# Norm factor kept in PSUM, half 1's product beside it, one set of PSUM banks with fixed homes at the passages, mask cast on ScalarE

## The chip, the cores and the metric

The kernel runs on one core of a Trainium2 chip. Its engines each work through their own queue of instructions in order: TensorE (PE, matrix products; its weight loads are listed as PEld), VectorE (DVE), ScalarE (ACT), GpSimd (POOL) and SyncE (SP, which issues the DMAs). The metric is the device time of one execution in microseconds (us); the median of several executions is compared.

## The reference

One inference step of a two-layer backbone on 640 tokens (128 context tokens, 512 latent ones) of width 1024. Layer 0 is an FFN half-step, a mixer (windowed attention beside a gated linear attention, one input and one output projection) and another FFN half-step; layer 1 is an FFN half-step, a chunked gMLP mixer and another FFN half-step. Each sub-layer is wrapped alike, and it is this wrapping that the change touches:

```python
def rmsnorm(x, g):
    xf = x.astype(jnp.float32)
    y = xf * lax.rsqrt(jnp.mean(xf * xf, axis=-1, keepdims=True) + EPS)
    return (y * g.astype(jnp.float32)).astype(x.dtype)

def sub_in(x, mod, i, g_pre):
    return rmsnorm(x, g_pre) * (1 + mod[:, i, 1][:, None]) + mod[:, i, 0][:, None]

def sub_out(x, y, mod, i, g_post, coef):
    return x + coef * mod[:, i, 2][:, None] * rmsnorm(y, g_post)

def macaron_ffn(x, mod, i, g_pre, g_post, wg, wu, wd):
    h = sub_in(x, mod, i, g_pre)
    y = (jax.nn.silu(h @ wg) * (h @ wu)) @ wd
    return sub_out(x, y, mod, i, g_post, FFN_RESIDUAL)
```

So between the last product of one sub-layer and the first of the next stand a norm of y, a gated addition to x, a norm of x and a scaling.

## The kernel before

The activations x and y lie transposed in SBUF, 128 partitions by 8 chunks (KD) of 1024 features by 640 tokens. The tokens are cut into two halves: half 0 has 384, half 1 has 256, and these are two pieces of 128 with different gates (context and latent). Products are made in full precision from split operands: an activation is hh + hl, a weight tile whl holds its rounded value and the rest, and each 128x128 piece takes three matmuls (hh and hl with the rounded weight, hh with the rest). Weights stream from HBM through two raw buffers, are cast by ACT (line 100) and their rest is made by DVE (line 101). All code is recorded and put in order by a list scheduler, engine by engine, so the order on an engine isn't that of the text.

From one sub-layer to the next ("passage") the work is this. `tail` makes the last products and evacuates them into y; `chain`, once for each half, makes the norm factor (`rstd`: a matmul with ones sums the squares, ACT takes Ln and Exp), then for each chunk runs three stages, each one step behind the other: `f_t` multiplies y by gate and factor in place (line 428), `f_x` adds y to x (line 464) and has ACT make hh (line 435), `f_l` makes hl on DVE (line 440). Squares of the new x and a second `rstd` follow. `head` makes four products jointly (`gemm_joint`, chunk by chunk over four PSUM banks) for half 0 while the chains run, evacuates each as a product with the norm factor (`normed`, line 606), makes the later products, and does the same for half 1. Ahead of a mixer `renorm` normalises x once more, with the same helper (line 428, reading x) and hh, hl at lines 494 and 498.

PSUM has eight banks of 128 x 512 floats. Outside of the passages `ps()` takes from a ring of eight. `split_psum` closes the pool and opens one with two rings of four, "ps" and "sd" (with four dummy matmuls); `whole_psum` in `head` closes that again and opens a ring of eight, right before the joint products of half 1, so the first of these must wait until every bank of the old pool has been read. Two of the five passages (after out_proj) have no split: there the ring of eight stays.

Five passages are spoken of: P1 into mixer 0 (about 480 to 525 us), P2 from out_proj into the next FFN (857 to 902), P3 into layer 1's first FFN (1300 to 1342), P4 into mixer 1 (1742 to 1790) and P5 from its out_proj into the last FFN (1948 to 1995). In P1 the DVE queue also holds the cast of a mask for the mixer (line 901) and memsets (line 882).

Of the kernel before, what the change touches and what calls it, by code (L numbers as in the profile page):

```python
# [8 lines left out]
F32 = mybir.dt.float32  # L9
# [3 lines left out]
AF = mybir.ActivationFunctionType  # L13
# [4 lines left out]
P = 128  # L18
# [120 lines left out]
class Kern:  # L139
# [18 lines left out]
    def ps(self):  # L158
        if self.spare:
            return self.sd()  # L160
        return self.pp.tile([P, 512], F32, name=self.nm("ps"), tag="ps", bufs=8 - self.n_sd)

    def sd(self):

        return self.pp.tile([P, 512], F32, name=self.nm("sd"), tag="sd", bufs=self.n_sd)

    def open_psum(self, n_sd=0):
        self.n_sd, self.spare = n_sd, False
        self.g_ps = self.tc.tile_pool(name=self.nm("psum"), bufs=8, space=PSUM)
        self.pp = self.g_ps.__enter__()  # L170
# [12 lines left out]

# [267 lines left out]
    def chain(self, half, cur, nxt):  # L451
# [3 lines left out]
        o, n = HALF[half]  # L455
        self.rstd(half, 0, late=half == 1)
        yield

        def f_t(m):
            self.scaled(half, self.y, *cur, 2, m)  # L460

        def f_x(m):
            xs = self.x[:, m, o:o + n]
            nc.vector.tensor_add(xs, xs, self.y[:, m, o:o + n])  # L464
            if nxt is None:
                nc.sync.dma_start(out=self.O["x"][:, m, o:o + n], in_=xs)
            else:
                self.h_hi(half, *nxt, m)
# [12 lines left out]
        self.rstd(half, 2 if half and nxt != (0, 1) else 0, late=True)  # L481
        yield
# [48 lines left out]
    def tail(self, unit, n_blocks, cur, nxt, mod=()):  # L531
# [17 lines left out]
        for m in range(both, KD):  # L549
            unit(m, 1, wis)  # L550
            if nxt is not None:
                ws.pump(wis[-1] + (m + 1) * n_blocks // KD - both)
            st = min(11 - done, 1 if nxt is not None else LAST_STEPS[m])
            self.step(ch[0], st)
            done += st
        self.step(ch[0], 11 - done)
        return ch

    def head(self, ch, n_a, joint, unit, evac, nxt=None):
# [13 lines left out]
        for i in range(10):  # L573
            self.step(ch[1], 1)
# [277 lines left out]
    def mixer0(self, ch):  # L852
# [18 lines left out]
        def evac1(i, half, ps):  # L871
# [932 lines left out]
```

## Time and profile before

| | |
|---|---|
| time, three executions | 2420.77, 2416.78, 2415.56 us; median 2416.78 |
| the profiled execution | 2414.18 us, span 2412.4 us, mean granted clock 0.987 |
| busy share of the span | PE 96%, PEld 94%, DVE 77%, ACT 54%, POOL 14% |
| busy us | PE 2325.1, DVE 1851.1, ACT 1298.3, POOL 331.2 |
| chain that ended last, by engine | PE 74%, DVE 16%, DMA 4%, ACT 3%, issue 2%, POOL 1% |

PE is the engine on which the time lies; a busy share is an average over stages, and the stretches in which PE stands are short. They are found in the list of waits, placed by the timeline, and then the queue of the engine that PE waited for is read in the same stretch.

### The profile page before, as it was taken

The numbers are of one execution on the slowest core, as the hardware profiler recorded it, in microseconds if no ns is written. First come the engines' busy times: TensorE is split into PE (matmuls) and PEld (weight loads), VectorE is DVE, ScalarE is ACT, GpSimd is POOL, SyncE is SP. The second block draws the span as 40 slices with busy tenths as digits, with TensorE's granted clock in tenths as the row PEclk, the third lists the DMA queues.
The fourth block names the chain that finished last, engine by engine and source line by source line (L and its number), as shares of the span: only waits on it lengthen the run. The fifth ranks groups of instructions, "written<-read, shape, count | busy, mean of one in ns | idle before, by whom it ended". The sixth has DMA issues, their size and how long they took to land.

```text
span 2412.4 us, 40072 instructions
## 1 busy us (share of the span) xinstructions
PE 2325.1 (96%) x15528; PEld 2265.1 (94%) x15528; DVE 1851.1 (77%) x3315; ACT 1298.3 (54%) x2669; POOL 331.2 (14%) x289
## 2 busy tenths in 40 slices
PE   7899999989999999999999899999989999999998
PEld 5799999989898899999999899999978899999998
DVE  8888888795956698887886688787794787765574
ACT  4565455565446456554556465455573356554555
POOL 5200000140503330000004000000131540000002
PEclk9999999999999999999999999999999999999999
DMA  8333544431030343353543333443434343332322
GB/s 300 97 114 127 171 158 133 169 129 60 10 92 31 135 136 109 129 168 103 175 129 134 105 114 127 145 149 109 169 128 138 116 133 108 108 114 68 100 97 105
DMA packets 87569, 297.85 MB, mean 123 GB/s; under 512 B 9681, under 2 KB 15313, under 8 KB 84305
## 3 DMA queue, kind: packets, MB, share of 16 engines
q1 hardware_dynamic: 86082, 292.07, 37.2%
q8 instruction: 121, 1.98, 0.3%
q10 hardware_dynamic: 864, 2.17, 0.3%
q0 software_dynamic: 432, 1.05, 0.2%
q14 instruction: 70, 0.57, 0.1%
HBM read 276.25 MB, written 19.01 MB: 122 GB/s over the span
## 4 chain that ended last, share of the span: by engine, by line
PE 74%; DVE 16%; DMA 4%; ACT 3%; issue 2%; POOL 1%; SPq 0%; DVEq 0%; ACTq 0%; POOLq 0%
PE ps L201 38%; PE sd L201 35%; DVE hl L440 2%; DVE junk L328 2%; DVE whl L101 2%; DVE y L428 2%; DVE x L464 1%; DMA wmod<-in_wmod 1%; DMA b<-xspill 1%; ACT whl L100 1%; DMA wraw<-in_wgu 1%; DMA cbc<-in_cc 1%; DVE dm L369 1%; DVE tmp L606 0%; DVE cv L1419 0%
## 5 line engine op out<-in xcount | busy, mean ns | idle before, releaser
L201 PE MATMUL ps<-hh,whl 128*128 128x320 f32 (+4 forms) x4080 | 941.0, 315 | 38.2 <-DVE tmp L606 30.5
L101 DVE TENSOR_TENSOR whl<-wraw,whl 128x1024 fp32r<-128x1024 f32 (+3 forms) x552 | 532.8, 970 | 294.9 <-ACT whl L100 283.1
L201 PEld LDWEIGHTS ps<-hh,whl 128*128 128x128 f32 x4080 | 701.7, 191 | 43.6 <-ACT tmc L405 12.1
L201 PE MATMUL ps<-hl,whl 128*128 128x320 f32 (+4 forms) x2040 | 637.0, 312 | 16.1 <-DVE hl L440 14.7
L100 ACT CAST whl<-wraw 128x1024 fp32r<-128x1024 f32 (+3 forms) x552 | 462.2, 839 | 337.8 <-issue 124.2
L201 PE MATMUL sd<-g,whl 128*128 128x384 f32 (+1 forms) x3264 | 480.6, 308 | 0.3 <-DVE g L687 0.3
L201 PEld LDWEIGHTS sd<-g,whl 128*128 128x128 f32 x3264 | 477.0, 188 | 2.8 <-DVE g L687 1.1
L412 POOL TENSOR_TENSOR acc<-acc,tmc 128x384 f32<-128x384 f32 (+1 forms) x154 | 178.2, 1159 | 1748.8 <-ACT tmc L405 1735.6
L201 PEld LDWEIGHTS ps<-hl,whl 128*128 128x128 f32 x2040 | 391.5, 192 | 21.5 <-DVE hl L440 16.9
L201 PE MATMUL sd<-th,whl 128*128 128x320 f32 x2448 | 381.4, 308 | 1.3 <-ACT sd L690 1.1
L201 PEld LDWEIGHTS sd<-th,whl 128*128 128x128 f32 x2448 | 364.8, 187 | 2.1 <-ACT sd L690 1.6
L328 DVE SCALAR_TENSOR_TENSOR junk<-wmod,cbc 128x1024 bf16<-128x1024 f32 x258 | 326.7, 1266 | 30.8 <-DMA wmod<-in_wmod 20.4
L201 PE MATMUL sd<-hh,whl 128*128 128x320 f32 (+1 forms) x592 | 144.1, 314 | 0.0
L201 PEld LDWEIGHTS ps<-g,whl 128*128 128x128 f32 x960 | 140.0, 188 | 1.5 <-issue 1.5
L201 PE MATMUL ps<-g,whl 128*128 128x384 f32 (+1 forms) x960 | 140.8, 308 | 0.0
L826 ACT COPY y<-sd 128x384 f32<-128x384 f32 (+1 forms) x192 | 80.6, 424 | 103.5 <-PE sd L201 103.3
L201 PEld LDWEIGHTS sd<-hh,whl 128*128 128x128 f32 x592 | 101.9, 188 | 0.6
L435 ACT ACTIVATE hh<-x,dm 128x128 fp32r<-128x128 f32 (+1 forms) x144 | 63.3, 468 | 62.8 <-DVE x L464 43.9
L428 DVE SCALAR_TENSOR_TENSOR y<-y,dm,rstd 128x128 f32<-128x128 f32 (+1 forms) x128 | 70.7, 584 | 32.0 <-ACT rstd L399 32.0
L440 DVE SCALAR_TENSOR_TENSOR hl<-x,dm,hh 128x128 fp32r<-128x128 f32 (+1 forms) x144 | 90.2, 656 | 2.1 <-ACT hh L435 1.8
L201 PE MATMUL sd<-hl,whl 128*128 128x320 f32 (+1 forms) x296 | 91.3, 308 | 0.0
L797 ACT COPY sd<-y 128x384 f32<-128x384 f32 (+1 forms) x192 | 81.1, 434 | 17.2 <-DVE tmp L701 14.1
(251 smaller groups left out, 2599.2 us busy)
## 6 DMA issues: line engine op xcount, KB each, us to landing
wraw<-in_wgu SPq DMA_DIRECT2D x170, 512.0 KB, 3.7
wmod<-in_wmod SPq DMA_DIRECT2D x130, 512.0 KB, 4.1
wraw<-in_wd SPq DMA_DIRECT2D x64, 320.0 KB, 3.2
xspill<-x SPq DMA_DIRECT2D x12, 1280.0 KB, 4.5
x<-xspill SPq DMA_DIRECT2D x12, 1280.0 KB, 8.6
wraw<-in_wd SPq DMA_DIRECT2D x32, 384.0 KB, 3.8
wraw<-in_wdl SPq DMA_DIRECT2D x24, 512.0 KB, 3.7
b<-xspill SPq DMA_DIRECT2D x16, 640.0 KB, 4.5
```

The lines of the kernel that those rows point to most:

```text
L100: k.nc.scalar.copy(w[:, 0, c], raw)
L101: k.nc.vector.tensor_sub(w[:, 1, c], raw, w[:, 0, c])
L201: self.nc.tensor.matmul(out, lhsT, rhs, start=start, stop=stop, **more)
L328: ins = nc.vector.scalar_tensor_tensor(junk, w, 1.0, self.c_bc[:, cond, :], op0=ALU.mult, op1=ALU.mult, accum_out=out)
L369: nc.vector.tensor_add(out, raw, bc(b))
L412: self.nc.gpsimd.tensor_add(acc, acc, t)
L428: self.nc.vector.scalar_tensor_tensor(self.y[:, m, a:a + ln], src[:, m, a:a + ln], self.mcol(lay, s, which, m, cond), r[:, a - o:a - o + l ...
L435: self.nc.scalar.activation(self.hh[:, k, 2 + a:2 + a + ln], self.x[:, k, a:a + ln], AF.Copy, scale=self.mcol(lay, s, 1, k, cond))
L440: self.nc.vector.scalar_tensor_tensor(self.hl[:, k, 2 + a:2 + a + ln], self.x[:, k, a:a + ln], self.mcol(lay, s, 1, k, cond), self.hh[:, k ...
L464: nc.vector.tensor_add(xs, xs, self.y[:, m, o:o + n])
L797: nc.scalar.copy(seeds[m, half][:, :n], self.y[:, m, o:o + n])
L826: nc.scalar.copy(ys, ps[:, :n])
```

## The change

The first norm factor of `chain` is written by Exp into the PSUM bank that holds the sum ("ps" for half 0, "sd" for half 1), and the two stages of gating and adding become one: the gate step (line 460 of the changed kernel) takes the factor from PSUM. For half 1 its product goes into columns 256 to 512 of the same bank, and the add (line 464) reads it there; for half 0 it stays in y. The pipeline has two stages, so a chain has one step less (10 for 11, and 9 for 10 in `head`). One pool with the rings "ps" and "sd", four banks each, lives all through the kernel; outside of the split `ps()` alternates between them. In `head` the joint products of half 0 take three "ps" banks and an "sd" one, the later products of half 0 "sd" alone, the joint products of half 1 four "ps" banks. `whole_psum` is gone; `split_psum` only sets a flag and makes its four dummies. The mask cast moves from DVE to ACT, three small memsets from DVE to POOL.

```diff
     def ps(self):
-        if self.spare:
-            return self.sd()
-        return self.pp.tile([P, 512], F32, name=self.nm("ps"), tag="ps", bufs=8 - self.n_sd)
+        if self.only:
+            return self.bank(self.only)
+        if not self.split:
+            self.turn_ps ^= 1
+            return self.bank("sd" if self.turn_ps else "ps")
+        return self.bank("ps")
+
+    def bank(self, tag):
+        return self.pp.tile([P, 512], F32, name=self.nm(tag), tag=tag, bufs=4)
...
     def split_psum(self):
-        self.close(self.g_ps)
-        self.open_psum(4)
-        for _ in range(self.n_sd):
+        self.split = True
+        for _ in range(4):
             self.mm(self.sd(), self.hh[0:1, 0, 0:P], self.hh[0:1, 0, 0:512])
-
-    def whole_psum(self):
-        self.close(self.g_ps)
-        self.open_psum()
...
-        nc.scalar.activation(r, r, AF.Exp, scale=-0.5)
-        return r
+        out = ps[:, :n] if keep else r
+        nc.scalar.activation(out, r, AF.Exp, scale=-0.5)
+        return ps if keep else r
...
-        self.rstd(half, 0, late=half == 1)
+        r = self.rstd(half, 0, bank="sd" if half else "ps", keep=True)
         yield
-        def f_t(m):
-            self.scaled(half, self.y, *cur, 2, m)
-
         def f_x(m):
+            t = r[:, 512 - n:] if n <= 256 else self.y[:, m, o:o + n]
+            for a, ln, cond in SEGS[half]:
+                nc.vector.scalar_tensor_tensor(t[:, a - o:a - o + ln], self.y[:, m, a:a + ln],
+                                               self.mcol(*cur, 2, m, cond), r[:, a - o:a - o + ln],
+                                               op0=ALU.mult, op1=ALU.mult)
             xs = self.x[:, m, o:o + n]
-            nc.vector.tensor_add(xs, xs, self.y[:, m, o:o + n])
+            nc.vector.tensor_add(xs, xs, t)
...
-        yield from self.pipeline(KD, [(0, f_t), (1, f_x), (2, f_l)])
+        yield from self.pipeline(KD, [(0, f_x), (1, f_l)])
...
-        pss = self.gemm_joint(wis[:joint], self.hacts(0, True), between)
+        self.split = False
+        pss = self.gemm_joint(wis[:joint], self.hacts(0, True), between, banks=["ps"] * 3 + ["sd"])
...
-        self.spare = self.n_sd > 0
+        self.only = "sd"
         for i in range(joint, n_a):
             unit(i, 0, wis[i])
+        self.only = None
...
-        if self.n_sd:
-            self.whole_psum()
-        pss = self.gemm_joint(wis[:joint], self.hacts(1), late)
+        pss = self.gemm_joint(wis[:joint], self.hacts(1), late, banks=["ps"] * joint)
...
-                nc.vector.memset(lr[32:33, o:o + n], 1.0)
+                nc.gpsimd.memset(lr[32:33, o:o + n], 1.0)
...
-        nc.vector.tensor_copy(mask, mraw)
+        nc.scalar.copy(mask, mraw)
```

Three places of the new order follow. The first is the PE queue in P1, where the last product of half 0 ends and the joint products of half 1 begin; ps_... and sd_... are banks by their numbers, whl108 to whl111 the four weight tiles. Before:

```order
L201 MATMUL sd_497_5304<-hh_67,whl112_5036 128x386
L201 MATMUL ps_500_5337<-hh_67,whl108_4880 128x256 [waits DVE_49,PE_49,Activation_49]
L201 MATMUL ps_500_5337<-hl_68,whl108_4880 128x256
L201 MATMUL ps_500_5337<-hh_67,whl108_4880 128x256
L201 MATMUL ps_501_5338<-hh_67,whl109_4910 128x256
L201 MATMUL ps_501_5338<-hl_68,whl109_4910 128x256
L201 MATMUL ps_501_5338<-hh_67,whl109_4910 128x256
```

In the changed kernel at the same place:

```order
L199 MATMUL sd_495_5300<-hh_67,whl112_5035 128x386
L199 MATMUL ps_497_5329<-hh_67,whl108_4876 128x256 [waits Activation_49]
L199 MATMUL ps_497_5329<-hl_68,whl108_4876 128x256 [waits DVE_49]
L199 MATMUL ps_497_5329<-hh_67,whl108_4876 128x256
L199 MATMUL ps_498_5330<-hh_67,whl109_4908 128x256 [waits DVE_49,PE_49]
L199 MATMUL ps_498_5330<-hl_68,whl109_4908 128x256
L199 MATMUL ps_498_5330<-hh_67,whl109_4908 128x256
L199 MATMUL ps_499_5331<-hh_67,whl110_4941 128x256 [waits DVE_49,PE_49]
```

and the first use of the fourth bank, 24 matmuls behind the start:

```order
L199 MATMUL ps_498_5330<-hh_67,whl109_4908 128x256
L199 MATMUL ps_498_5330<-hl_68,whl109_4908 128x256
L199 MATMUL ps_498_5330<-hh_67,whl109_4908 128x256
L199 MATMUL ps_500_5332<-hh_67,whl111_5002 128x256 [waits DVE_49,PE_49]
L199 MATMUL ps_500_5332<-hl_68,whl111_5002 128x256
L199 MATMUL ps_500_5332<-hh_67,whl111_5002 128x256 x2
```

Before, the first matmul of half 1 carried all of the waits, and the other banks none; now bank 1 waits for ACT and for its hl, and each of the other banks has a wait of its own for one evacuation.

The second is the DVE queue in P1 where half 1's chain begins (x, y, dm are activations and gates, hl the low part, lmask the mask). Before:

```order
L440 SCALAR_TENSOR_TENSOR hl_68<-x_428_4562,dm_71,hh_67 128x384 x2
L901 CAST lmask_5595<-mraw_5593 128x896
L428 SCALAR_TENSOR_TENSOR y_5_81<-y_5_81,dm_71,rstd_77 128x128 x4
L464 TENSOR_TENSOR x_428_4562<-x_428_4562,y_5_81 128x256
L428 SCALAR_TENSOR_TENSOR y_5_81<-y_5_81,dm_71,rstd_77 128x128 x2
L464 TENSOR_TENSOR x_428_4562<-x_428_4562,y_5_81 128x256
L440 SCALAR_TENSOR_TENSOR hl_68<-x_428_4562,dm_71,hh_67 128x128 x2
L428 SCALAR_TENSOR_TENSOR y_5_81<-y_5_81,dm_71,rstd_77 128x128 x2
L464 TENSOR_TENSOR x_428_4562<-x_428_4562,y_5_81 128x256
L440 SCALAR_TENSOR_TENSOR hl_68<-x_428_4562,dm_71,hh_67 128x128 x2
L874 TENSOR_SCALAR wb0_5096<-ps_480_5101 128x2
L428 SCALAR_TENSOR_TENSOR y_5_81<-y_5_81,dm_71,rstd_77 128x128 x2
```

In the changed kernel:

```order
L437 SCALAR_TENSOR_TENSOR hl_68<-x_426_4558,dm_71,hh_67 128x384
L460 SCALAR_TENSOR_TENSOR sd_486_5174<-y_4_81,dm_71,sd_486_5174 128x128 x2
L464 TENSOR_TENSOR x_426_4558<-x_426_4558,sd_486_5174 128x256
L460 SCALAR_TENSOR_TENSOR sd_486_5174<-y_4_81,dm_71,sd_486_5174 128x128
L437 SCALAR_TENSOR_TENSOR hl_68<-x_426_4558,dm_71,hh_67 128x128
L460 SCALAR_TENSOR_TENSOR sd_486_5174<-y_4_81,dm_71,sd_486_5174 128x128
L437 SCALAR_TENSOR_TENSOR hl_68<-x_426_4558,dm_71,hh_67 128x128
L464 TENSOR_TENSOR x_426_4558<-x_426_4558,sd_486_5174 128x256
L460 SCALAR_TENSOR_TENSOR sd_486_5174<-y_4_81,dm_71,sd_486_5174 128x128
L437 SCALAR_TENSOR_TENSOR hl_68<-x_426_4558,dm_71,hh_67 128x128
L460 SCALAR_TENSOR_TENSOR sd_486_5174<-y_4_81,dm_71,sd_486_5174 128x128
L437 SCALAR_TENSOR_TENSOR hl_68<-x_426_4558,dm_71,hh_67 128x128
```

The cast has left the queue; the gate steps read and write bank sd_486 instead of y, and the adds follow them more closely.

The third is the PE queue in P2, where half 0's second and third joint banks are begun behind out_proj. Before:

```order
L201 MATMUL ps_1011_9084<-hh_67,whl137_8907 128x386
L201 MATMUL ps_1011_9084<-hl_68,whl137_8907 128x386
L201 MATMUL ps_1011_9084<-hh_67,whl137_8907 128x386
L201 MATMUL ps_1012_9085<-hh_67,whl138_8942 128x386 [waits Activation_49]
L201 MATMUL ps_1012_9085<-hl_68,whl138_8942 128x386
L201 MATMUL ps_1012_9085<-hh_67,whl138_8942 128x386 [waits DVE_49]
```

In the changed kernel:

```order
L199 MATMUL ps_1008_9076<-hh_67,whl137_8899 128x386 [waits Activation_49]
L199 MATMUL ps_1008_9076<-hl_68,whl137_8899 128x386
L199 MATMUL ps_1008_9076<-hh_67,whl137_8899 128x386
L199 MATMUL ps_1009_9077<-hh_67,whl138_8936 128x386 [waits Activation_49]
L199 MATMUL ps_1009_9077<-hl_68,whl138_8936 128x386
L199 MATMUL ps_1009_9077<-hh_67,whl138_8936 128x386 [waits DVE_49]
L199 MATMUL sd_1010_9078<-hh_67,whl139_8974 128x386
```

Before, the third bank's wait was for the cast of its weight tile alone (line 100). Now the second bank has a wait for a copy of ACT (line 1351, 1350 before), and the third waits for the copy of the very last out_proj product, which stands a few matmuls ahead on PE; the fourth, in the "sd" ring, begins without a wait.

## Rows read from the trace of the kernel before

**Rows 1.** Waits of PE: line waited for, us in total, times, longest us

```profile
PE ps L201 <- DVE tmp L606: 30.5, 3, 11.5
...
PE sd L201 <- DVE tmp L606: 4.6, 4, 1.7
```

**Rows 2.** Timeline of PE: start us, us, instruction, count, [idle before <- releaser]

```profile
525.10 0.55 PE L201 MATMUL ps<-hh,whl 128*128 128x256 f32 x1 [10.58 <-DVE tmp L606]
...
1341.44 0.55 PE L201 MATMUL ps<-hh,whl 128*128 128x256 f32 x1 [8.36 <-DVE tmp L606]
...
1787.89 0.55 PE L201 MATMUL ps<-hh,whl 128*128 128x256 f32 x1 [11.53 <-DVE tmp L606]
```

**Rows 3.** Stretches: us, busy of PE, PEld, DVE, ACT, POOL, PEclk, DMA, GB/s

```profile
525.20:532.60 7.40, 7.40 (x49) 7.40 (x50) 7.40 (x15) 5.09 (x9) 0.81 (x2) 0.78 0.67 205
1341.50:1350.20 8.70, 8.70 (x50) 8.67 (x51) 1.07 (x2) 0.51 (x1) 0.00 (x0) 0.65 0.01 2
1787.90:1795.40 7.50, 7.50 (x49) 7.50 (x50) 7.50 (x13) 4.81 (x9) 2.64 (x3) 0.77 0.28 114
```

**Rows 4.** Timeline of DVE in P1 (x2: two executions in a row)

```profile
506.47 1.44 DVE L901 CAST lmask<-mraw 128x896 uint8<-128x896 f32 x1
507.82 0.60 DVE L428 SCALAR_TENSOR_TENSOR y<-y,dm,rstd 128x128 f32<-128x128 f32 x2
...
519.25 0.61 DVE L428 SCALAR_TENSOR_TENSOR y<-y,dm,rstd 128x128 f32<-128x128 f32 x2
519.77 0.42 DVE L464 TENSOR_TENSOR x<-x,y 128x256 f32<-128x256 f32 x1
520.11 1.08 DVE L440 SCALAR_TENSOR_TENSOR hl<-x,dm,hh 128x128 fp32r<-128x128 f32 x2
```

**Rows 5.** DVE by line and shape, 480.3 to 525: count | busy us, mean ns

```profile
L428 DVE SCALAR_TENSOR_TENSOR y<-y,dm,rstd 128x384 f32<-128x384 f32 x8 | 6.7, 853 | 0.0
L440 DVE SCALAR_TENSOR_TENSOR hl<-x,dm,hh 128x128 fp32r<-128x128 f32 x16 | 6.7, 461 | 0.0
...
L428 DVE SCALAR_TENSOR_TENSOR y<-x,dm,rstd 128x384 f32<-128x384 f32 x1 | 0.6, 602 | 0.0
```

**Rows 6.** Lines 606 and 464 over the span: ns min/median/max, forms

```profile
L606 DVE TENSOR_TENSOR tmp<-ps,rstd x89: 414/425/555, 95.3 to 2033.1; 128x256 f32<-128x256 f32 x49, 128x384 f32<-128x384 f32 x40
...
L464 DVE TENSOR_TENSOR x<-x,y x88: 407/545/1374, 481.9 to 2399.5; 128x384 f32<-128x384 f32 x48, 128x256 f32<-128x256 f32 x40
```

**Rows 7.** Timeline of DVE in an FFN, a dependent pair and an independent one

```profile
173.46 0.49 DVE L701 TENSOR_TENSOR tmp<-sd,tmp 128x320 f32<-128x320 f32 x1
173.98 0.49 DVE L685 TENSOR_TENSOR tmp<-tmp,tmc 128x320 f32<-128x320 f32 x1
...
175.53 0.48 DVE L687 TENSOR_TENSOR g<-tmp,g 128x320 fp32r<-128x320 f32 x1
175.93 0.48 DVE L685 TENSOR_TENSOR tmp<-tmp,tmc 128x320 f32<-128x320 f32 x1
```

**Rows 8.** Timeline of DVE in P3 and in P4

```profile
1334.56 0.54 DVE L606 TENSOR_TENSOR tmp<-ps,rstd 128x384 f32<-128x384 f32 x1
...
1771.97 1.10 DVE L428 SCALAR_TENSOR_TENSOR y<-y,dm,rstd 128x128 f32<-128x128 f32 x1
```

**Rows 9.** Timelines of PE and of ACT in P2

```profile
865.67 0.52 PE L201 MATMUL ps<-hh,whl 128*128 128x386 f32 x2
...
867.46 0.62 PE L201 MATMUL ps<-hh,whl 128*128 128x386 f32 x2 [0.56 <-DVE whl L101]
...
867.90 1.05 ACT L100 CAST whl<-wraw 128x1024 fp32r<-128x1024 f32 x1 [0.98 <-DMA wraw<-in_wgu]
...
869.70 0.36 ACT L1350 COPY y<-ps 128x256 f32<-128x256 f32 x1
```

**Rows 10.** Timelines of PE and of ACT in P5

```profile
1960.61 0.52 PE L201 MATMUL ps<-hh,whl 128*128 128x386 f32 x2
...
1961.04 0.37 ACT L1350 COPY y<-ps 128x256 f32<-128x256 f32 x1
```

More of the change, by code (lines that the diff above doesn't have):

```diff
@@ L158, in ps @@
     def ps(self):
-        if self.spare:
-            return self.sd()
-        return self.pp.tile([P, 512], F32, name=self.nm("ps"), tag="ps", bufs=8 - self.n_sd)
-    def sd(self):
[L165 to L170, printed above, removed]
+        if self.only:
[6 more added lines that the diff above has]
+        return self.pp.tile([P, 512], F32, name=self.nm(tag), tag=tag, bufs=4)
+    def sd(self):
+        return self.bank("sd")
     def split_psum(self):
-        self.close(self.g_ps)
-        self.open_psum(4)
-        for _ in range(self.n_sd):
+        self.split = True
+        for _ in range(4):
             self.mm(self.sd(), self.hh[0:1, 0, 0:P], self.hh[0:1, 0, 0:512])
-    def whole_psum(self):
-        self.close(self.g_ps)
-        self.open_psum()
     def tmp(self, tag="tmp"):
@@ L221, in gemm, with gemm_joint @@
         return self.gemm_joint([wi], acts)[0]
-    def gemm_joint(self, wis, acts, hook=None, where=None, onto=None):
-        pss = onto or [self.ps() for _ in wis]
-        more = {"skip_group_check": True} if onto else {}
+    def gemm_joint(self, wis, acts, hook=None, where=None, banks=None):
+        pss = [self.bank(b) for b in banks] if banks else [self.ps() for _ in wis]
         n = acts[0][0].shape[-1]
@@ L234, in gemm_joint @@
                 wi, c = where(i, k) if where else (wis[i], k)
-                self.passes(ps[:, :n], self.ws.get(wi), acts[k], c, k == 0 and not onto, k == K - 1, **more)
+                self.passes(ps[:, :n], self.ws.get(wi), acts[k], c, k == 0, k == K - 1)
         return pss
@@ L272, in setup @@
         self.g_ring, self.ring = self.pool("ring")
-        self.open_psum()
+        self.split, self.only, self.turn_ps = False, None, 0
+        self.g_ps = self.tc.tile_pool(name="psum", bufs=8, space=PSUM)
+        self.pp = self.g_ps.__enter__()
         c = self.cons
@@ L378, in mcol, with rstd @@
         return self.dm[:, j:j + 1]
-    def rstd(self, half, table, more=None, late=False):
+    def rstd(self, half, table, more=None, bank=None, keep=False):
         nc = self.nc
         n = HALF[half][1]
-        self.spare = late and self.n_sd > 0
-        ps = self.ps()
-        self.spare = False
+        ps = self.bank(bank) if bank else self.ps()
         mm = self.nc.tensor.matmul(ps[:, :n], self.ones, self.accs[half], start=True, stop=more is None)
@@ L480, in chain @@
         yield from self.pipeline(KD, [(0, f_s)])
-        self.rstd(half, 2 if half and nxt != (0, 1) else 0, late=True)
+        self.rstd(half, 2 if half and nxt != (0, 1) else 0, bank="sd" if half else "ps")
         yield
@@ L552, in tail @@
                 ws.pump(wis[-1] + (m + 1) * n_blocks // KD - both)
-            st = min(11 - done, 1 if nxt is not None else LAST_STEPS[m])
+            st = min(10 - done, 1 if nxt is not None else LAST_STEPS[m])
             self.step(ch[0], st)
             done += st
-        self.step(ch[0], 11 - done)
+        self.step(ch[0], 10 - done)
         return ch
@@ L568, in between @@
             self.step(ch[0], 1)
-        pss = self.gemm_joint(wis[:joint], self.hacts(0, True), between)
+        self.split = False
+        pss = self.gemm_joint(wis[:joint], self.hacts(0, True), between, banks=["ps"] * 3 + ["sd"])
         self.step(ch[0], 99)
         todo = list(range(joint))
-        for i in range(10):
+        for i in range(9):
             self.step(ch[1], 1)
```

## The prediction

> **What bounds the kernel now.** I read the profile in this order: busy shares, waits of TensorE (PE), its timeline where the large waits end, the windows behind these, then the DVE queue in the same places. PE is busy for 96% of the span (the table above), so time can come only from the few places where it stands. The waits view puts 30.5 us, in three pieces, on the evacuations of line 606, and another 4.6 us in four pieces on the same line for the "sd" banks [rows 1]. The timeline places the three: PE stands 10.58 us until 525.10, 8.36 us until 1341.44 and 11.53 us until 1787.89 [rows 2]. I call these passages P1 (into mixer 0), P3 (into the second layer's first FFN) and P4 (into mixer 1). Each time PE has finished half 0's joint products and wants the first bank of half 1; the bank pool has been closed and opened again, so the first matmul waits for the last evacuation of all. Behind each stall the granted clock is below full: 0.78, 0.65 and 0.77 over 7.40, 8.70 and 7.50 us [rows 3].
>
> **The change part by part.**
>
> *Pool no longer closed: the three stalls.* In the order of the changed kernel half 1's first bank waits for an early Ln and for its hl operand; banks 2, 3 and 4 wait for the first, second and third evacuation (now line 607), one each. So what must be found is when these three stand in the DVE queue against when PE asks.
>
> P1. DVE begins half 1's chain at 507.82, right behind the mask cast of 506.47 [rows 4]. The cast moves to ScalarE: 1.35 us. Half 0's eight gate steps averaged 853 ns against 602 ns for the same form undisturbed [rows 5]. The new step takes its factor from PSUM; steps with a PSUM source (line 606) lie between 414 and 555 ns over 89 executions, those with SBUF sources alone (line 464) between 407 and 1374 [rows 6], so I take it as undisturbed: 8 x 0.25 = 2.0 us. Half 1 begins at 507.82 - 1.35 - 2.0 = 504.5 (506.5 if the new step is stretched too). Ahead of the third evacuation now stand 14 gate steps, 7 adds, 12 hl steps, 3 tiny ones of 0.07 and 2 evacuations. By their starts a pair of gate steps takes 0.52 us and an add 0.34 [rows 4], hl goes as the gate step: 14 x 0.26 + 7 x 0.33 + 12 x 0.26 + 0.2 + 3 x 0.47 = 10.7 us to its end. The hl steps averaged 461 ns [rows 5] where of an undisturbed gate pair each takes 0.34 us (0.60 busy in all, starts 0.26 apart) [rows 4]: 16 x 0.12 = 1.9. An add can now follow directly on the product that it reads; such a pair costs 0.52 us from start to start (173.46 to 173.98) against 0.40 for an independent one (175.53 to 175.93) [rows 7]: 0.12 for each of four adds that stand directly behind their product ahead of that evacuation, 0.5. Third evacuation done at 504.5 + 13.1 = 517.6. PE ends half 0 at 525.10 - 10.58 = 514.52, has 24 matmuls of banks 1 to 3 (0.12 us each at full clock) and asks for bank 4 at 517.4: a stall of 0.2 (0 to 2.2) instead of 10.58.
>
> P3. The third evacuation starts at 1334.56 [rows 8], earlier in the new order; PE ends half 0 at 1333.08 and asks 2.9 us later. Nothing is left (0 to 1) of 8.36.
>
> P4. Half 1 begins at 1771.97 [rows 8], minus 2.0 as in P1, so 1770.0. Counted along the new order as above, the first evacuation ends some 7.5 us later, 1777.5, the third at 1779.6. PE ends half 0 at 1776.36, has nine matmuls of bank 1 ahead (to 1777.4), and wants bank 4 at about 1779.9. I take 1.0 (0 to 3) instead of 11.53.
>
> *The clock behind them.* 7.40 x 0.22 + 8.70 x 0.35 + 7.50 x 0.23 = 6.4 us of full-speed work were lost [rows 3]. With PE not standing I take all of it back.
>
> *Four dummies for the "sd" ring.* They waited 4.55 us for the last evacuations of half 0. Now these are made one half-1 product (24 x 0.12 = 2.9 us) earlier, against a longest wait of 1.7 [rows 1]: 4.3 back (3.8 to 4.55).
>
> *Four-deep "ps" ring: a new wait, P2.* From out_proj into the FFN the order now has half 0's third joint bank wait for the ScalarE copy (line 1351) of the last out_proj product. Before, eight banks hid it. PE reaches that matmul at 865.85 (the second of the pair at 865.67); the copy starts at 869.70 behind a weight cast that waited for its DMA until 867.90, and an hh cast [rows 9]. DVE's gain moves the weight slot, so the DMA and the copy, earlier by up to 2 us: copy done between 868.1 and 870.06; I take 869.1. Stall 3.2, in place of the 0.56 at 867.46 [rows 9]: 2.6 lost. Behind PE's wait all of the joint products queue, and their evacuations. For the clock I take 1.0 (0 to 1.7, the loss behind P1). Together 3.6 (1.7 to 5.9). At the second such place, P5, the copy ends at 1961.41 against PE at 1960.79 (second of the pair at 1960.61) [rows 10]: 0.2 (0 to 0.6).
>
> *What the mixers give back.* In the windows behind P1 and P4 DVE is busy all of the time, 7.40 of 7.40 and 7.50 of 7.50 us, behind P3 only 1.07 of 8.70 [rows 3]. When PE comes 12 us earlier, the renorm steps and weight casts must too. In P1 DVE has 2.5 us of chain left at 517.6 and 8 half-0 renorm pairs of 2 x 0.60: done at 529.7. PE's 96 + 24 half-1 matmuls end at 529.1. The two come out together; I take 2.0 in mixer 0 (0 to 8.8) and 1.0 in mixer 1 (0 to 11).
>
> *The rest.* The mask cast (1.4 us on DVE) costs ScalarE about what its weight cast of 1024 columns does, 1.05 [rows 9]; it lies under ScalarE's waits for DVE's adds; without that cover +1.0, once. Memsets on GpSimd, busy 0.81 of 7.40 us behind P1 [rows 3], hide there. Exp into PSUM replaces Exp into SBUF, in the same place.
>
> [...]
>
> **Sum.** 30.5 + 6.4 + 4.3 = 41.2 us back. Lost: 0.2 + 1.0 + 3.6 + 0.2 + 2.0 + 1.0 = 8.0. Net 33.2. The profiled execution took 2414.18 us, so 2381.0; it lies 2.6 under the median of 2416.78, which becomes **2383.6**.
>
> **The rivals.**
>
> *DVE becomes the bound in the mixers.* If DVE really has no room, PE gains in P1 only what DVE gains (1.35 + 2.0 of 12.2) and in P4 2.0 of 13.3: 8.8 + 11 lost where I took 3 + 1.2. With P2 at its worst, too, about 2402. For it: the full windows. Against: part of DVE's work there is only late because it waits for PE itself. I set the case at half to all of that, 2391 to 2402.
>
> *P2 costs nothing.* The cast's DMA comes earlier and the stall vanishes with its clock: 2383.6 - 3.6 - 3 (mixers at zero) = 2377. Against: the copy is 3.9 us late now.
>
> *The change misses.* If PE still stood for the last evacuation, only DVE's 3.4 us at P1 would come back: about 2413. Against: the waits that stand in the order.
>
> *Slower: half 1's chain on one bank.* Sixteen gate steps and eight adds per passage write and read one PSUM bank, each add right behind its product, the next product right behind the add. If such a step costs more than now, DVE delays PE by 24 times that in each of five passages. The present gain is 33.2, 6.6 for each, and evacuations have some 7 us of slack before PE suffers more than the old stall: from 13.6/24 = 0.57 us per step on, the kernel is slower; at 0.75 it is 5 x 24 x 0.18 = 22 us, 2438. For: no row shows a vector step that writes PSUM and is read at once. Against: 0.12 for the pair in SBUF [rows 7].
>
> **How the numbers follow.** Forecast, 2378 to 2391: 0.58. DVE bound, 2391 to 2403: 0.22. P2 free and mixers clean, under 2378: 0.10. Missed, 2409 to 2417: 0.04. Slower, over 2422: 0.06. The range 2376 to 2402 holds the forecast, most of the second case and half of the third. 0.2% is 4.8 us, about what a measurement of this kernel tells from no change. Faster by more than that: 0.58 + 0.22 + 0.10 + 0.02 = 0.92, less 0.02 for unknown parts, 0.90; within 0.04; slower 0.06.
>
> **What would show it.** Right: in the waits of PE no piece above 3 us on line 607; clock 1.00 behind P1, P3, P4; a wait of 2 to 4 us on the copy at line 1351 near 868. Wrong: PE waiting in mixer 0 for hl or weight subtractions (DVE bound), or gate steps into PSUM well above 0.6 us (slower).

## The result, and the profile after

The changed kernel takes 2383.31 us (median of 4, 2380.68 to 2384.27) against 2416.54 us before (median of 4); the ratio is 0.9857 with a 95% interval of 0.984 to 0.9875. Measured a second time it was 2382.72 us, ratio 0.9867 (0.9851 to 0.9883). The forecast was 2383.6. The profiled execution took 2384.27 us, 29.9 less than the 2414.18 of before, so in the two traces the gain to be explained is 30, not 33.2. The second measurement of the same kernel left a trace as well, called the repeat below; by the spans its gain is 32.0. Part of how close the forecast came is scatter of the executions.

First the page of the changed kernel, span and busy shares:

```profile
span 2382.4 us, 40080 instructions
...
PE 2327.0 (98%) x15528; PEld 2267.3 (95%) x15528; DVE 1835.2 (77%) x3312; ACT 1298.1 (54%) x2670; POOL 335.7 (14%) x291
```

PE does the same 15528 matmuls in the same busy time (2327.0 for 2325.1); what went is time in which it stood. The waits of PE after the change (line waited for, us in total, times, longest us):

```profile
PE sd L199 <- DVE hl L437: 13.9, 5, 4.9
PE ps L199 <- ACT hh L445: 6.0, 1, 6.0
PE ps L199 <- ACT y L1351: 4.4, 1, 4.4
...
PE ps L199 <- ACT rstd L394: 1.4, 1, 1.4
PE ps L199 <- DVE tmp L607: 1.2, 2, 0.7
```

These answer to [rows 1]: 30.5 us in three pieces on the evacuations became 1.2 in two, and the 4.6 of the "sd" banks are gone. Two waits are new: 4.4 us on the copy at line 1351 and 1.4 on the Ln at line 394. (The waits on hl and hh lie in the first 80 us in both kernels.) The timeline of PE places them:

```profile
517.68 0.35 PE L199 MATMUL ps<-hh,whl 128*128 128x256 f32 x1 [0.73 <-DVE tmp L607]
...
859.67 0.69 PE L199 MATMUL ps<-hh,whl 128*128 128x386 f32 x1 [4.45 <-ACT y L1351]
...
1758.13 0.39 PE L199 MATMUL ps<-hh,whl 128*128 128x256 f32 x1 [1.41 <-ACT rstd L394]
...
1760.05 0.43 PE L199 MATMUL ps<-hh,whl 128*128 128x256 f32 x1 [0.43 <-DVE tmp L607]
```

The windows behind P1, P2 and P4 (the columns of [rows 3]; the last figures are the granted clock, the share of DMA and GB/s):

```profile
517.80:525.00 7.20, 7.10 (x56) 6.84 (x57) 7.20 (x19) 6.30 (x14) 1.47 (x2) 1.00 0.46 184
859.70:868.40 8.70, 8.70 (x33) 8.70 (x34) 8.70 (x9) 4.70 (x9) 7.80 (x6) 0.64 0.42 137
1758.20:1765.50 7.30, 6.87 (x43) 6.69 (x44) 7.30 (x25) 7.19 (x18) 2.37 (x4) 0.77 0.44 182
```

The clock is full behind P1, but P2 now has the slow stretch, and P4 has kept its own. The repeat shows that these two clocks aren't fixed by the kernel. PE stood 4.49 us at P2 there, and at P4 1.01 and 0.44; at P4 the wait, then the windows behind P2 and P4, in the repeat:

```profile
1756.45 0.39 PE L199 MATMUL ps<-hh,whl 128*128 128x256 f32 x1 [1.01 <-ACT rstd L394]
```

```profile
860.30:869.00 8.70, 8.70 (x42) 8.70 (x43) 8.70 (x9) 4.73 (x9) 7.74 (x6) 0.83 0.43 130
1756.50:1763.80 7.30, 6.86 (x55) 6.68 (x56) 7.30 (x25) 7.18 (x18) 2.37 (x4) 1.00 0.44 182
```

Behind almost the same waits the granted clock was 0.64 and 0.77 in one execution and 0.83 and 1.00 in the other.

Where the 30 us come from is read by pairing the matmuls of two traces and following how much earlier the same matmul starts; the last column does this with the repeat:

| place | forecast, us gained | read from the two traces | from the repeat |
|---|---|---|---|
| P1, stall and clock | 12.0 | 10.9 | 11.7 |
| mixer 0 | -2.0 | -0.6 | -0.7 |
| P2 | -3.6 | -5.3 | -3.8 |
| four dummies | 4.3 | 4.8 | 3.7 |
| P3, stall and clock | 11.4 | 11.3 | 11.3 |
| P4, stall and clock | 12.3 | 9.4 | 11.3 |
| mixer 1 | -1.0 | -0.4 | -0.6 |
| P5 | -0.2 | -0.4 | -0.4 |
| the rest | 0 | 0.3 | -0.5 |
| sum | 33.2 | 30.0 | 32.0 |

(The forecast's clock terms stand with their passages.) Two executions of one kernel differ by 0.8 us at P1, 1.5 at P2, 1.9 at P4 and 1.1 at the dummies; a difference of that size between two single traces is not told from scatter.

### The profile page after: what moved, and what is told of

Read it like the earlier page. It is cut to its first block, busy times and chain, and to the rows that moved or that the text cites. A ratio compares the mean times of both kernels' runs of the same rounds, so it can differ in the third digit from the quotient of the medians.

```text
span 2382.4 us, 40080 instructions
## 1 busy us (share of the span) xinstructions
PE 2327.0 (98%) x15528; PEld 2267.3 (95%) x15528; DVE 1835.2 (77%) x3312; ACT 1298.1 (54%) x2670; POOL 335.7 (14%) x291
## 4 chain that ended last, share of the span: by engine, by line
PE 80%; DVE 11%; DMA 3%; ACT 3%; issue 2%; POOL 0%; SPq 0%; DVEq 0%; ACTq 0%; POOLq 0%
PE sd L199 48%; PE ps L199 31%; DVE junk L327 2%; DVE whl L101 2%; DVE hl L437 1%; DMA wmod<-in_wmod 1%; ACT whl L100 1%; DMA wraw<-in_wgu 1%; DVE x L464 1%; DMA cbc<-in_cc 1%; DVE dm L368 1%; DVE cv L1420 0%; DVE nm L1283 0%; DVE y L460 0%; DMA wraw<-in_wd 0%
## 5 line engine op out<-in xcount | busy, mean ns | idle before, releaser
L199 PE MATMUL ps<-hh,whl 128*128 128x320 f32 (+4 forms) x3056 | 703.7, 308 | 13.2 <-ACT hh L445 6.0
L199 PEld LDWEIGHTS ps<-hh,whl 128*128 128x128 f32 x3056 | 519.9, 190 | 15.9 <-ACT hh L445 6.1
L199 PE MATMUL ps<-hl,whl 128*128 128x320 f32 (+4 forms) x1528 | 465.5, 305 | 0.4 <-DVE hl L446 0.4
L199 PE MATMUL sd<-hh,whl 128*128 128x320 f32 (+4 forms) x1616 | 421.2, 327 | 0.9 <-ACT hh L432 0.6
L199 PEld LDWEIGHTS sd<-hh,whl 128*128 128x128 f32 x1616 | 290.9, 191 | 4.5 <-ACT hh L432 2.4
L199 PEld LDWEIGHTS ps<-hl,whl 128*128 128x128 f32 x1528 | 291.8, 191 | 1.6 <-DVE hl L446 0.7
L199 PE MATMUL sd<-hl,whl 128*128 128x320 f32 (+4 forms) x808 | 262.6, 325 | 14.8 <-DVE hl L437 13.9
L199 PEld LDWEIGHTS sd<-hl,whl 128*128 128x128 f32 x808 | 154.6, 191 | 18.9 <-DVE hl L437 15.8
```

The costliest lines, as they stand in the source:

```text
L199: self.nc.tensor.matmul(out, lhsT, rhs, start=start, stop=stop, **more)
```

## The experiments

Theory: the closed pool made the three stalls; a ring of four, short of one bank, makes the new one at P2; DVE has no room at P1 and P4. Rivals: the shorter DVE work carries the gain; PE is held at P2 by something else anyway; DVE does have room at P1 and P4.

**The bank part alone.** The factor stays in SBUF with three stages, the cast and memsets stay on DVE; only the pool and the homes are those of the change.

```diff
-        r = self.rstd(half, 0, bank="sd" if half else "ps", keep=True)
+        self.rstd(half, 0, bank="sd" if half else "ps")
...
-        yield from self.pipeline(KD, [(0, f_x), (1, f_l)])
+        yield from self.pipeline(KD, [(0, f_t), (1, f_x), (2, f_l)])
```

> The bank part of the change alone: one pool, fixed homes; the norm factor in SBUF, three stages, mask cast and memsets on DVE as before. My theory (the closed pool made the three stalls, and PE now waits for the first to third evacuation): most of the gain stays, P3 loses nothing of it (evacuations there are done 6.8 us ahead of PE), P1 is later by the cast 1.35, the stretched half-0 steps 2.0 and 0.4 of half 1, P4 by 2.0 + 1.9; with the clock behind P1 some 1.6: 2383.3 + 3.7 + 3.9 + 1.6 = 2392 us (2388 to 2397). Rival, that the shorter DVE work of the PSUM factor carries the gain: 2405 us or more, with stalls of over 7 us at P1 and P4.

Measured: 2392.12 us, ratio 0.9906 (0.9891 to 0.992). So 23 of the 33 us come from the banks alone. PE's timeline in P1, P2's half 1 and P4:

```profile
514.68 0.39 PE L199 MATMUL ps<-hh,whl 128*128 128x256 f32 x1 [1.00 <-ACT rstd L394]
516.72 0.55 PE L199 MATMUL ps<-hh,whl 128*128 128x256 f32 x1 [1.42 <-DVE tmp L605]
521.05 0.35 PE L199 MATMUL ps<-hh,whl 128*128 128x256 f32 x1 [1.30 <-DVE tmp L605]
...
889.33 0.35 PE L199 MATMUL ps<-hh,whl 128*128 128x256 f32 x1 [2.53 <-DVE tmp L605]
...
1763.07 0.58 PE L199 MATMUL ps<-hh,whl 128*128 128x256 f32 x1 [4.96 <-ACT rstd L394]
```

Short waits at P1 and 4.96 us at P4, in size as expected, though the one at P4 ends with the Ln at line 394 and not with an evacuation. But the sum was right by luck: against the changed kernel's trace P1 lost 4.1 and P4 3.9, P3 another 1.3 where I had nothing, and P2 won 6.6 and lost 2.8 of it again at line 605. The stall on the copy of the last out_proj product isn't there at all, though the ring is as deep. The difference between the two kernels that bears on this is the factor: where it stays in its "ps" bank through half 0's chain, the ring has three banks left, where it does not, four.

**The factor alone.** Factor and product in PSUM with two stages, in the kernel before with its pools.

```diff
-        self.rstd(half, 0, late=half == 1)
+        r = self.rstd(half, 0, late=half == 1, keep=True)
...
-        yield from self.pipeline(KD, [(0, f_t), (1, f_x), (2, f_l)])
+        yield from self.pipeline(KD, [(0, f_x), (1, f_l)])
```

> The factor and half 1's product in PSUM with two stages, the pool still closed before half 1, cast and memsets on DVE. My theory: PE still waits for the last evacuation, which comes earlier by what DVE saves, 2.0 of half 0 and some of half 1 at P1 and P3, 3 at P4: three stalls of 8.5, 6.4 and 8.5, 2416.5 - 7 = 2409 us (2406 to 2414). Rival, the saving is hidden: three stalls of 30 us in all, 2416. Rival, the DVE saving carries the gain: below 2395.

Measured: 2422.61 us, ratio 1.0033 (1.0021 to 1.0045): slower than before, which no theory had. Waits and timeline of PE:

```profile
PE ps L201 <- DVE y L463: 11.3, 3, 4.0
PE ps L201 <- DVE tmp L609: 11.0, 2, 6.6
PE ps L201 <- DVE x L467: 8.6, 1, 8.6
```

```profile
501.33 0.56 PE L201 MATMUL ps<-hh,whl 128*128 128x386 f32 x1 [3.73 <-DVE y L463]
...
527.10 0.55 PE L201 MATMUL ps<-hh,whl 128*128 128x256 f32 x1 [6.64 <-DVE tmp L609]
```

The three stalls at half 1 did shrink (6.64, 4.41 and 8.62 for the 10.58, 8.36 and 11.53 of [rows 2]), but PE now also stands 3.6 to 4.0 us in front of half 0: line 463 is the gate step that reads the factor, and with the factor in one "ps" bank the fourth joint bank has to wait until half 0's last gate step has read it. The factor in PSUM is thus worth having only with homes of three "ps" and one "sd" bank; the two parts of the change need each other. The same shortage makes P2's stall; the next two runs test that. (Factor in PSUM and two stages for three came together in every run; no run separates these two.)

**P2 with two and two.** In the passages without a split half 0's joint products take two banks of each ring.

```diff
+        homes = ["ps"] * 3 + ["sd"] if self.split else ["ps"] * 2 + ["sd"] * 2
         self.split = False
-        pss = self.gemm_joint(wis[:joint], self.hacts(0, True), between, banks=["ps"] * 3 + ["sd"])
+        pss = self.gemm_joint(wis[:joint], self.hacts(0, True), between, banks=homes)
```

> As the changed kernel, but in the passages without a split (P2, P5) half 0's joint products take two ps and two sd banks instead of three and one. My theory (P2 stands for the copy of the last out_proj product because the third ps bank is that product's): the stall of 4.45 us shrinks to 0 to 1.4 us (now behind a copy that ends 2.9 us earlier), the granted clock behind it goes from 0.64 to 1.00 (3.1 us): 2383.3 - 6 = 2377 us (2375.5 to 2380). Rival, that PE at P2 is held by hh, hl or weights which come no earlier: stall moves to a DVE or ACT wait of the same size, 2383 us.

Measured: 2380.76 us, ratio 0.9856 (0.984 to 0.9873). The stall went and PE won 6.1 us on the changed kernel's trace within P2, but 3.6 of it came back there and 1.2 in P5: the "sd" ring, too, is now short, and half 0's later products wait 1.68 us in P2 and 1.02 in P5 for an evacuation of it. PE in P2 and P5:

```profile
855.68 0.44 PE L199 MATMUL sd<-hh,whl 128*128 128x386 f32 x1 [0.94 <-DVE whl L101]
...
880.18 0.41 PE L199 MATMUL sd<-hh,whl 128*128 128x386 f32 x1 [1.68 <-DVE tmp L608]
...
1951.55 0.41 PE L199 MATMUL sd<-hh,whl 128*128 128x386 f32 x1 [1.02 <-DVE tmp L608]
```

**P2 with the other ring first.** out_proj starts its alternation with the other ring, so that its last product lies in an "sd" bank.

```diff
         mod.pop(0)()
-        return self.tail(unit, KD, (lay, 1), (lay, 2), mod)
+        self.turn_ps ^= 1
+        ch = self.tail(unit, KD, (lay, 1), (lay, 2), mod)
+        self.turn_ps ^= 1
+        return ch
```

> As the changed kernel, but out_proj begins its alternation with the other ring, so that its last product lies in an sd bank and the third ps bank of the joint products waits for the last product but one, whose copy ended at 856.73 us instead of 859.61. My theory (the ring of four and that copy make the stall at P2): 4.45 becomes 1.5 us and the clock behind it 0.64 becomes 1.00, without the later waits on sd banks that the version with two ps and two sd banks had (1.7 at P2, 1.0 at P5): 2383.3 - 5.5 = 2378 us (2376 to 2380.5). Rival, hh, hl or weights hold PE at P2 anyway: another wait of 3 us or more in its place, 2382 to 2384 us.

Measured: 2376.92 us, ratio 0.9841 (0.9827 to 0.9854), the lowest median of all. The wait and the window behind it:

```profile
856.29 0.44 PE L199 MATMUL ps<-hh,whl 128*128 128x386 f32 x1 [1.49 <-ACT y L1351]
```

```profile
856.30:865.00 8.70, 8.70 (x50) 8.70 (x50) 8.70 (x11) 5.86 (x11) 6.69 (x5) 1.00 0.40 125
```

4.45 us became 1.49, as expected from the copy one product earlier, and the clock 0.64 became 1.00. In P2 PE wins 4.6 us on the changed kernel's first trace, and 1.9 more at P4, where the clock is 1.00 here. But the unchanged kernel's repeat also has 1.00 at P4 and wins the same 1.9 there, and it has 0.83 at P2: the 1.9 isn't due to this edit, and of the clock at P2 only a part can be.

**The changed kernel once more**, beside that version:

> The changed kernel once more, beside the kernel before, in as many rounds as the version with the other ring first in out_proj had (2376.92 us, ratio 0.9841). If that version's gain of some 6 us at P2 is real, this one gives 2383 us, a ratio of 0.9865, with P2's stall of 4 to 5 us and a clock of about 0.64 behind it. If it was chance of the run: 2377 to 2379 us.

Measured: 2382.72 us, ratio 0.9867 (0.9851 to 0.9883), with 4.49 us at P2 and a clock of 0.83 behind it. The intervals around 0.9841 and 0.9867 overlap by a little. Of the 5.4 us between the two traces 3.1 lie in P2, about what the shorter wait explains (1.49 for 4.49); 2.3 more lie ahead of P1, where the kernels are the same. So the other ring is worth some 3 us; the rest of the 6 is not shown to come from it.

**More DVE work in half 1's chain.** Each gate step of half 1 is executed twice, or, in the second version, for every second chunk.

```diff
-            for a, ln, cond in SEGS[half]:
+            for a, ln, cond in SEGS[half] * (2 if half else 1):
```

> As the changed kernel, but each of the 16 gate steps of half 1 in every passage is executed twice (the same values are written again): 16 x 0.26 = 4.2 us more of DVE in each passage. My theory: P2, P3 and P5 hide it (the evacuations are 6.8 us ahead of PE there), P1 and P4 do not: 14 x 0.26 = 3.7 at P1, 3.5 at P4, and 1.6 of clock behind P1: 2383.3 + 8.8 = 2392 us (2388 to 2395). Rival, DVE is the bound in all passages: 5 x 4.2 = 21, 2404 us. Rival, there is cover everywhere: 2383 us.

> As the changed kernel, but the gate steps of half 1 are executed twice for every second chunk alone: 2.1 us more of DVE in each passage, half of the dose that gave 10.4 us at P1 and 15 at P4 (25 in all). If the price is per microsecond of DVE (no cover): 12 us, 2396 us, half at each of the two. If it comes from a new order beyond a threshold (renorm steps put between the chain's): either 3 to 5 us, 2387 us, or the whole 25.

Measured: 2408.49 us (ratio 0.997, 0.9958 to 0.9982) and 2396.08 us (0.9917, 0.9904 to 0.9931), so 25.2 us for the whole dose and 12.8 for half of it: in sum the price goes with the dose, and neither forecast of a threshold came. P2, P3 and P5 do hide the work (about 1 us each at most). P1 and P4 charge about 11 and 13 us for 4.2 us of DVE (10.4 and 15 in the second expectation were a rougher reading of the same trace). With half of the dose P1 itself charges 3.5 and P4 4.6, about a third; another 4.2 come in mixer 0, most of them where PE stands a little longer for an operand that DVE makes (0.70 us where the changed kernel has 0.14) and has a low clock behind that:

```profile
559.16 0.38 PE L199 MATMUL sd<-ldh,ut 128*128 128x256 f32 x1 [0.70 <-DVE ldh L936]
```

```profile
558.50:567.80 9.30, 8.64 (x44) 8.64 (x45) 7.30 (x16) 4.38 (x18) 0.00 (x0) 0.64 0.31 89
```

So place by place the price isn't shown to be proportional. It isn't the evacuations that PE waits for where the dose is whole. The timeline of PE in P1 with all gate steps doubled, and the window around it:

```profile
523.39 0.75 PE L199 MATMUL ps<-hh,whl 128*128 128x256 f32 x4 [1.45 <-ACT hh L432]
...
526.91 0.75 PE L199 MATMUL ps<-hh,whl 128*128 128x256 f32 x4 [1.64 <-ACT hh L432]
...
531.05 1.22 PE L199 MATMUL ps<-hh,whl 128*128 128x256 f32 x4 [1.28 <-ACT hh L432]
...
534.43 1.22 PE L385 MATMUL sd<-acc,ones 128*128 128x256 f32 x2 [2.16 <-POOL acc L409]
```

```profile
519.00:541.00 22.00, 14.89 (x87) 13.28 (x85) 18.07 (x45) 11.77 (x31) 6.32 (x6) 0.77 0.25 97
```

Half 1's own chunks come late: the adds, and with them hh, stand behind the extra steps and between the renorm steps of half 0, PE stops at chunk after chunk, then for the sum of squares, and the clock falls to 0.77. In the order of the changed kernel DVE is just fast enough for PE at these two places, and no faster.

**The cast and memsets back on DVE.**

```diff
-        nc.scalar.copy(mask, mraw)
+        nc.vector.tensor_copy(mask, mraw)
```

> As the changed kernel, with the mask cast and the memsets on DVE again. My theory after the doubled gate step (no cover on DVE in P1, and a microsecond of DVE there costs PE more than one): the cast of 1.44 us comes back at P1 alone with a factor of 1 to 2.5: 1.4 to 3.6 us, 2385 to 2387 us. Rival (it is hidden in the changed kernel, where half 1 waits for its factor from ScalarE for 1.42 us at 505.11): 2383.3 us and an offset at P1 below 0.5 us.

Measured: 2384.28 us, ratio 0.9869 (0.9856 to 0.9882), 1.0 us over the changed kernel, which isn't told from nothing. In the trace PE is 2.1 us later by the middle of mixer 0: it loses 3.3 there, at the same wait for line 936 (0.70 us) and a clock of 0.62 over the 9.0 us behind it. By the end of P4 it is ahead again, but 2.2 of that come in P4, where the unchanged kernel's own two traces differ by 1.9. The run leaves this part of the change open at a size of 0 to 3 us.

**Half 1's product in y.**

```diff
-            t = r[:, 512 - n:] if n <= 256 else self.y[:, m, o:o + n]
+            t = self.y[:, m, o:o + n]
```

> As the changed kernel, but half 1's product goes to y in SBUF as half 0's does; the factor stays in PSUM. If the store to PSUM and the read from it cost nothing of their own but keep the add clear of GpSimd (adds with a PSUM source lay between 401 and 422 ns, 48 with SBUF sources reached 1382): 8 adds per passage longer by up to 0.1 at P1 and P4, 2383.3 to 2386 us. If a PSUM store with a read right behind it costs something (the slower rival), this version is faster by 0.1 x 24 x 2 = 5 us: 2378 us.

Measured: 2388.1 us, ratio 0.9889 (0.9875 to 0.9902), so the product in PSUM is worth some 5 us. In P1 it isn't the adds that got longer, as I had it, but the hl steps (in P4 six of the adds did, too: 493 ns between 1720 and 1765, where the changed kernel's eight took 412). DVE by line and shape, first of this version (504 to 530), then of the changed kernel (505 to 525); count, busy us, mean ns:

```profile
L437 DVE SCALAR_TENSOR_TENSOR hl<-x,dm,hh 128x128 fp32r<-128x128 f32 x16 | 8.8, 562 | 0.0
L460 DVE SCALAR_TENSOR_TENSOR y<-y,dm,sd 128x128 f32<-128x128 f32 x16 | 4.8, 337 | 1.4 <-ACT sd L396 1.4
...
L464 DVE TENSOR_TENSOR x<-x,y 128x256 f32<-128x256 f32 x8 | 3.3, 414 | 0.0
```

```profile
L437 DVE SCALAR_TENSOR_TENSOR hl<-x,dm,hh 128x128 fp32r<-128x128 f32 x16 | 6.1, 383 | 0.2
L460 DVE SCALAR_TENSOR_TENSOR sd<-y,dm,sd 128x128 f32<-128x128 f32 x16 | 5.6, 349 | 1.5 <-ACT sd L396 1.4
...
L464 DVE TENSOR_TENSOR x<-x,sd 128x256 f32<-128x256 f32 x8 | 3.3, 410 | 0.0
```

With the store to PSUM a gate step took 12 ns more (349 for 337) and the add no more (410 for 414), while the hl steps, which touch SBUF alone, took 562 ns for 383. The timelines of DVE and GpSimd show where that lies. An addition of GpSimd beside an hl step, in this version, and beside an add that reads PSUM, in the changed kernel:

```profile
511.23 0.87 POOL L409 TENSOR_TENSOR acc<-acc,tmc 128x256 f32<-128x256 f32 x1 [1.66 <-ACT tmc L402]
511.42 0.83 DVE L437 SCALAR_TENSOR_TENSOR hl<-x,dm,hh 128x128 fp32r<-128x128 f32 x1
```

```profile
509.10 0.82 POOL L409 TENSOR_TENSOR acc<-acc,tmc 128x256 f32<-128x256 f32 x1 [4.48 <-ACT tmc L402]
509.24 0.41 DVE L464 TENSOR_TENSOR x<-x,sd 128x256 f32<-128x256 f32 x1
```

In this version seven of the sixteen hl steps take 807 to 877 ns, each beside at least 0.65 us of such an addition; the other nine take 340 to 348, beside 0.06 us at most. In the changed kernel the additions lie mostly beside steps with a PSUM operand, which keep their length, and two hl steps are stretched (786 and 503 ns); a third, at 516.40, lies beside 0.30 us of one and took 340 all the same.

**Three tries on top of the version with the other ring first.** Evacuations one step earlier; the second sum of half 0 in an "sd" bank ahead of the mixers; both, with the order ps, ps, sd, ps of the joint banks.

```diff
-EV = 3
+EV = 2
...
-        self.rstd(half, 2 if half and nxt != (0, 1) else 0, bank="sd" if half else "ps")
+        self.rstd(half, 2 if half and nxt != (0, 1) else 0, bank="sd" if half or nxt[1] == 1 else "ps")
...
-banks=["ps"] * 3 + ["sd"])
+banks=["ps", "ps", "sd", "ps"])
```

> The version with the other ring first in out_proj, and half 0's evacuations put one chain step earlier (EV = 2 for 3). If the second to fourth bank at P1 and P4 wait for evacuations that stand behind chain steps in the DVE queue: the pieces of 0.48 + 0.71 at P1 and 0.46 at P4 vanish, 1.7 us: 2376.9 - 1.5 = 2375.4 us. Rival (DVE has no cover there, so what comes earlier in the queue makes hl and hh of half 1 later): the waits on line 607 go and waits on hl or hh of the same size come, 2377 to 2380 us.

> The version with the other ring first in out_proj, and the second norm factor's sum of half 0 in an sd bank ahead of the mixers, so that half 1's first bank at P4 waits no longer for the Ln that reads that sum (1.07 us). My theory: the wait goes, but PE then comes 1.1 us earlier to the second bank's evacuation (0.46 now) and to half 1's hh and hl, and most of it returns there: 2376.2 to 2377 us. Rival: it was the only bound, 2375.5 us.

> Both together, and the joint products of half 0 in the order ps, ps, sd, ps, so that P2's bank behind the copy comes 0.5 us later. If evacuation, Ln and the copy are the bounds: 0.5 at P2, 1.2 at P1, 1.5 at P4: 2373.7 us. If DVE is: P2's 0.5 alone, 2376.4 us or more.

Measured: 2380.79, 2380.03 and 2382.04 us (ratios 0.9853, 0.9848 and 0.9858), none faster than without them; by their medians they are 3 to 5 us slower, but all of the intervals overlap with that of 0.9841. What was removed came back as another wait: with the earlier evacuations P1 waits 1.48 us for one and P4 1.47 for the Ln; with the sum moved, P4 has 0.94 us on hl and 0.53 on an evacuation in place of the Ln; with all three, hl (0.67) and the sum of squares (0.99). The tries agree with the doubled gate steps: at P1 and P4 DVE sets the pace, and these other orders of the same work gave PE nothing.

## Why the prediction was right, point by point

**The stalls at P1 and P3.** Right in mechanism and in size. At P1 the third evacuation was forecast to end at 517.6; the changed kernel's DVE:

```profile
505.11 0.75 DVE L460 SCALAR_TENSOR_TENSOR sd<-y,dm,sd 128x128 f32<-128x128 f32 x2 [1.42 <-ACT sd L396]
...
516.99 0.54 DVE L607 TENSOR_TENSOR tmp<-ps,rstd 128x384 f32<-128x384 f32 x1
```

It ends at 517.53. That it agrees to 0.1 us is luck, since errors in it cancel: the chain began at 505.1, not 504.5, because DVE was ready before ScalarE had written the factor and waited 1.42 us for it; the hl steps were stretched less (383 ns, not 461); and the sum charged that stretch to 16 hl steps where 12 stand ahead of this evacuation, 0.5 us too much. P3 had nothing left, as forecast.

**P4** gave 9.4 us for 12.3, and 11.3 in the repeat. Most of the 1.9 between these two executions of one kernel is the clock: 0.77 over 7.30 us, or 1.7 us, in the first, 1.00 in the second. The sign that I had named, a clock of 1.00 behind P4, was thus met in one trace of two. What is left is a mis-sized term: I moved the start of half 1's chain by the whole 2.0 us of half 0's shorter gate steps. In the trace it begins at 1751.91; with the 19.64 us by which PE is ahead there, that is 0.4 us earlier than 1771.97 in [rows 8] (0.8 in the repeat):

```profile
1751.91 0.75 DVE L460 SCALAR_TENSOR_TENSOR sd<-y,dm,sd 128x128 f32<-128x128 f32 x2 [0.57 <-ACT sd L396]
...
1759.35 0.55 DVE L607 TENSOR_TENSOR tmp<-ps,rstd 128x384 f32<-128x384 f32 x1
```

The gate steps did get shorter, 603 ns for 854, but DVE spent the difference on waits for ScalarE and on adds of 384 columns that were stretched more (959 ns for 888). So the first evacuation came late (waits of 0.43 and 0.44 us), and PE also met a wait that I had called early, on the Ln (1.41 and 1.01).

**P2** was right in its place and cause, too small in size: the stall was 4.45 and 4.49 us, for 3.2 and for the 2 to 4 that I had named as the sign; the clock cost 3.1 us in the first trace (0.64 over 8.70) and 1.5 in the repeat (0.83), for 1.0. (The upper end of its range, 5.9, leaves out the 0.56 that the stall replaces; it should have been 5.3.) The term that was mis-sized in both traces is how much earlier the copy comes:

```profile
857.52 1.05 ACT L100 CAST whl<-wraw 128x1024 fp32r<-128x1024 f32 x1 [0.79 <-DMA wraw<-in_wgu]
...
859.25 0.36 ACT L1351 COPY y<-ps 128x256 f32<-128x256 f32 x1
```

The copy ends at 859.61; with 10.8 us of lead that is 870.4, no earlier than before ([rows 9]: 870.06). The weight's DMA sets it, and DVE's gain does not reach that. I had also put the stall down to the ring of four alone; in the run of the bank part, a ring of four without the factor, it isn't there, so it takes the factor's bank, too.

**The dummies and the mixers.** The dummies gave 4.8 and 3.7 us (4.3 forecast). Mixers 0 and 1 took back 1.0 and 1.3 us where I had 3.0, and the rival in which DVE eats the gain there did not happen. The run with half of the doubled gate steps shows how near it was: 2.1 us more of DVE in the chain cost 3.5 in P1 and 4.2 in mixer 0.

**The slower rival** fell: gate steps that store to PSUM cost 349 ns, and the product in y was slower, not faster.

**The price of a PSUM operand.** Lines 460 and 464 of the changed kernel over the whole span (ns min/median/max):

```profile
L460 DVE SCALAR_TENSOR_TENSOR sd<-y,dm,sd x80: 339/350/358, 505.1 to 1958.2; 128x128 f32<-128x128 f32 x80
L460 DVE SCALAR_TENSOR_TENSOR y<-y,dm,ps x48: 599/602/616, 479.9 to 2367.1; 128x384 f32<-128x384 f32 x48
...
L464 DVE TENSOR_TENSOR x<-x,y x48: 543/614/1382, 480.9 to 2368.3; 128x384 f32<-128x384 f32 x48
L464 DVE TENSOR_TENSOR x<-x,sd x40: 401/411/422, 505.9 to 1958.7; 128x256 f32<-128x256 f32 x40
```

The gate step with its factor from PSUM takes 602 ns, what [rows 5] has for SBUF alone, and never more than 616. The sum had taken the step as undisturbed, and it was. The add with its product from PSUM takes 411 ns at the median; the shortest from SBUF alone, at the same 256 columns, took 407 [rows 6].

## What to carry to other kernels

A pool that is closed and opened again was a barrier on every buffer in it here (10.58, 8.36 and 11.53 us [rows 2]); one ring with fixed homes turns one wait for the last reader into waits for single ones, and here that alone was 23 us. Count the banks that live long before counting the ring: a tile kept through a stage (the factor) makes a ring of four a ring of three, and the shortage shows up elsewhere, at the last copy of the stage before. Where an engine off the critical path is just fast enough, a microsecond added to it can cost two or three, by late operands and by the clock behind the waits (11 and 13 us for 4.2 here); test that with a doubled step before rearranging its queue. And trace the same kernel twice before giving a cause to a difference of 2 us at one place: here the unchanged kernel differed by 1.9 at P4.

## What the runs showed of the hardware

- In the changed kernel the vector steps of lines 460 and 464 with a PSUM operand weren't stretched: 168 executions lie within 5% of their form's median (350, 602 and 411 ns), while adds of 384 columns from SBUF alone reached 1382 ns with a median of 614.
- The same kernel at the same place, with nearly the same waits, had two clocks in two executions: in P4 1.41 and 0.43 us with 0.77 over the 7.30 us behind the first, and 1.01 and 0.44 us with 1.00; in P2 4.45 us with 0.64 over 8.70 us, and 4.49 us with 0.83.
- In P1, with the product in y, hl steps with all operands in SBUF took 807 to 877 ns beside a GpSimd addition where the others took 340 to 348; in the changed kernel adds with one operand in PSUM kept 401 to 422 ns.
